# One cast and one subtraction per weight chunk, and GpSimd's elementwise work moved to VectorE and ScalarE, in a hybrid transformer block

## The chip, the core and the metric

The kernel runs on one core of a Trainium2 chip. The time is device microseconds of one execution. Its engines work in parallel, each through its own queue in order: TensorE (matmuls, and the loads of their stationary operand), VectorE, ScalarE, GpSimd, and SyncE, which here only issues transfers. In the profile they are PE and PEld, DVE, ACT, POOL and SP.

## What is computed

One layer on 256 tokens of width 2048, all in float32: a norm, one wide projection, four mixers (RWKV-7, RG-LRU, sparse attention "NSA", gated linear attention "GLA"), a gated sum of their outputs, an output projection with a residual, a second norm, and a feed-forward part with a causal convolution of three taps. In outline:

```
h = rms_norm(x);  p = h @ w_in
y_n = mixer_n(its columns of p)                      n = 0..3, each 256 x 512
m   = sum_n sigmoid(gate_n) * (y_n @ w_branch_n)     gate_n: 2048 columns of p
x2  = x + m @ w_out
u   = conv3(rms_norm(x2) @ w_up);  out = x2 + (silu(u1) * u2) @ w_down
```

The RWKV mixer needs, in each chunk of 64 tokens and each head, the inverse of a unit triangular matrix. It is solved by rows in two 32 x 32 blocks on each diagonal, and the corners are filled in by matmuls.

## The kernel before, in words

**The stream.** All activations are kept with channels on the 128 partitions and the 256 tokens along the free dimension. The weights (some 290 MB) are read once, in chunks of 128 x 1024 float32, each one transfer of 512 KB on SyncE's queue into a ring of five tiles `raw` (`stream`, line 300). A float32 product is made from rounded pieces: each weight is split into a high part `wh` and a low part `wl`. For each half chunk of 512 columns ScalarE casts `raw` to `wh` (line 327) and VectorE subtracts, `wl = raw - wh` (line 328). `wh` and `wl` are rings of six half chunks each (`BUFS`, line 1524). `stream` is a generator: it hands out blocks of 256 columns (512 in the three wide groups). The kernel does 1,096 such half chunks, in 548 chunks.

**The matmuls.** `group_A` takes 16 blocks or so (the contraction) and accumulates two tiles of 128 output channels in PSUM: for each block and tile one matmul of 512 columns with `wh` (both pieces of the activation) and one of 256 columns with `wl`. So a chunk of four blocks is 16 matmuls of 384 columns on average. Two accumulators of this kind alternate. Each group is then evacuated by ScalarE and VectorE (`fold`, `scaled`).

**The order.** The program order is: the projections of RWKV, its decay and solve (`rwkv_lora`, `rwkv_head`), the projections of RG-LRU and its recurrence (`lru`), the gates and branch products of RG-LRU (`merge(1, ...)`), with `rwkv_corners` called in the middle of them, after the third group of gates; then RWKV's chain of four chunks, GLA with its eight levels, its merge, NSA, the last two merges, the output projection, and the feed-forward part in three sections of 8, 7 and 7 units (`glu`), each followed by its part of `w_down`. A planner (the framework's, on modelled times) fixes the order of each engine's queue ahead of the run. It takes what is ready by priority: `load`, then `split`, then `evac`, then `mix` (all mixers' arithmetic), then `big` (the stream's matmuls); within a band in program order. `rwkv_corners` keeps its transpose of Z in program order on VectorE.

**GpSimd's share.** Helpers `tt` and `ts` run on VectorE unless given an engine. GpSimd gets:
- `rwkv_kk` (line 656): four scalings `kk` of 256 columns and the two products `k2` and `rk` of 1024 columns;
- `rwkv_blocks` (line 717): the solve, 31 steps of a product `ztmp` and a sum into `Z`, each of r x w columns with r = 31 - k, w = min(k + 1, 16) for k = 0..30, every one needing the one before. It begins with transfers of N (out to DRAM and back, on SyncE's queue) and ends with the store of `Z`, eight loads of `Zb` on the same queue and the transpose in `rwkv_corners`;
- `rwkv_chain` (line 820): the scaled state `sd`, in two of the four chunks;
- `gla` (line 1037): in each of eight levels one of the two products `qe` of 512 columns;
- `nsa` (line 1277): sixteen scalings of softmax rows `pt` of 128 or 256 columns;
- `branch` (line 1348): 24 additions of 512 columns into `merged`;
- and, not touched by the change, the sums of squares of the two norms (`norm_sum`), memsets, one-element copies ahead of loads, and some DMA issues.

Of the kernel before, what the change touches and what calls it, by code (L numbers as in the profile page):

```python
# [11 lines left out]
F32 = mybir.dt.float32  # L12
F32R = mybir.dt.float32r
U8 = mybir.dt.uint8
AF = mybir.ActivationFunctionType
ALU = mybir.AluOpType
MULT, ADD, SUB = ALU.mult, ALU.add, ALU.subtract
# [3 lines left out]
P = 128  # L21
# [204 lines left out]
class Kern:  # L226
# [73 lines left out]
    def stream(self, arr, c0, width, nblk):  # L300

        nc = self.nc
        nb, ns = 1024 // width, 512 // width
        for d in range(0, nblk, nb):
            if self.extras and not self.first and d % (self.every * nb) == 0:
                self.extras.pop(0)()
            self.nt += 1
            raw = self.pools["w"].tile([P, 1024], F32, tag="raw", bufs=BUFS["raw"], name=f"raw_{self.nt}")
            src = arr[c0 + d // nb]
            if self.first:  # L310
                with self.at("load"):
                    nc.sync.dma_start(raw[:, 0:512], src[:, 0:512])
                    nc.sync.dma_start(self.prm, self.A["prm"])
                self.extras.pop(0)()
                with self.at("load"):
                    nc.sync.dma_start(raw[:, 512:1024], src[:, 512:1024])
                self.first = False
            else:
                with self.at("load"):
                    nc.sync.dma_start(raw, src)  # L320
            for b in range(2):
                with self.at("split"):
                    self.nt += 1
                    wh = self.pools["w"].tile([P, 512], F32R, tag="wh", bufs=BUFS["wh"], name=f"wh_{self.nt}")
                    wl = self.pools["w"].tile([P, 512], F32R, tag="wl", bufs=BUFS["wl"], name=f"wl_{self.nt}")
                    rb = raw[:, b * 512:(b + 1) * 512]
                    nc.scalar.copy(wh, rb)  # L327
                    nc.vector.tensor_tensor(wl, rb, wh.bitcast(F32), op=SUB)  # L328
                for o in range(0, 512, width):
                    yield wh[:, o:o + width], wl[:, o:o + width]  # L330

    def acc(self):
        self.nt += 1
# [323 lines left out]
    def rwkv_kk(self):  # L657
        nc = self.nc
        hs = self.cst("hs")
        self.hs = hs  # L660
        kk = self.m4("kk")
        for j in range(4):
            nc.gpsimd.tensor_scalar(kk[:, j, :], self.rw_k[:, j, :], self.col("k_k", j), None, op0=MULT)
        sq = self.m4("kksq")
        self.act(sq, kk, AF.Square)

        def pre(out, ps):
            self.ts(out, ps, 1e-24, None, ALU.max)
            self.act(out, out, AF.Sqrt)

        def post(jp, pb):
            self.tt(kk[:, 2 * jp:2 * jp + 2, :], kk[:, 2 * jp:2 * jp + 2, :], pb, MULT)

        self.head_norm(sq, hs, pre, post)
        self.rw_kk = kk

        hka = self.sm([P, 4], "hka")
        self.ts(hka, self.col("k_a", 0, 4), 0.5, None, MULT)
        oka = self.sm([P, 4], "oka")
        self.ts(oka, hka, -1.0, 1.0, MULT, ADD)  # L680
        k2 = self.m4("k2")
        for j in range(4):
            self.act(k2[:, j, :], self.rw_tha[:, j, :], AF.Identity, scale=hka[:, j:j + 1], bias=oka[:, j:j + 1])
        self.tt(k2, k2, self.rw_k, MULT, nc.gpsimd)
        self.rw_k2 = k2
        bb = self.m4("bb")
        self.ts(bb, self.rw_tha, 0.5, 0.5, MULT, ADD)
        self.tt(bb, bb, kk, MULT)
        self.rw_b = bb
        rk = self.m4("rk")  # L690
        self.tt(rk, self.rw_r, k2, MULT, nc.gpsimd)
        self.rw_rk = rk

    def rwkv_ops(self, c):
# [19 lines left out]
    def rwkv_blocks(self, Ts):  # L714


        nc = self.nc
# [13 lines left out]
        nb = self.sb("mg", [P, 32, 32], F32, "N32")  # L731
        zb = self.m2("Z32", 32)
        tmp = self.m1("ztmp", 1)[:, 0, :]
        nc.sync.dma_start(self.flat(zb), self.A["z0"])
        for hf in range(2):
            for q in range(2):
                o = 64 * hf + 32 * q
                nc.sync.dma_start(nb[o:o + 32], nd.rearrange("u (a t) s -> (u a) t s", a=2)[:, 32 * q:32 * q + 32, 32 * q:32 * q + 32])
        for k in range(31):
            r, w = 31 - k, min(k + 1, 16)  # L740
            t = tmp[:, 0:r * w].rearrange("p (r w) -> p r w", r=r)
            self.tt(t, nb[:, k + 1:, k:k + 1].broadcast_to([P, r, w]), zb[:, k:k + 1, 0:w].broadcast_to([P, r, w]), MULT, nc.gpsimd)
            self.tt(zb[:, k + 1:, 0:w], zb[:, k + 1:, 0:w], t, ADD, nc.gpsimd)
        y = self.m4("Zb", 16)
        nc.gpsimd.memset(y, 0.0)
        nc.sync.dma_start(zd.rearrange("f q u a t s -> (f q u a) t s"), zb)
        for a in range(2):
            for q in range(2):
                for hf in range(2):
                    o, c0 = 64 * a + 32 * q, 32 * q + 16 * hf  # L750
# [67 lines left out]
    def rwkv_chain(self, c, T, st):  # L818
        nc = self.nc
# [19 lines left out]
        if c < 3:  # L839
            tk = T["tk"]  # L840
            ps = g4("S")
            for j in range(4):
                for par in range(2):
                    self.mm(ps[H[par], j, :], tk[:, par, j, :], uv[:, j, par, :])
            new = self.sb("st", [P, 4, 64], F32, "st")
            if st is None:
                nc.vector.tensor_copy(new, ps)
            else:
                sd = self.m1("sd")
                ec = self.rw_ec[:, :, c:c + 1]  # L850
                self.tt(sd, st, ec.broadcast_to([P, 4, 64]), MULT, nc.gpsimd)
                self.tt(new, sd, ps, ADD)
        ps = g4("Yo")
        for j in range(4):
# [182 lines left out]
    def gla(self):  # L1037
# [28 lines left out]
        for lv in range(8):  # L1066
# [6 lines left out]
            self.act(e, e, AF.Exp, scale=-1.0 / 16)  # L1073
            qe = self.m4("qe")
            self.tt(qe[:, 0:2, :], qk[:, 0:2, :], e, MULT)
            self.tt(qe[:, 2:4, :], qk[:, 2:4, :], e, MULT, nc.gpsimd)
            if lv == 6:
                for par in range(2):
                    h = H[par]
# [196 lines left out]
    def nsa(self):  # L1276
# [24 lines left out]
        for tt in range(2):  # L1301
# [19 lines left out]
            self.tt(lt, lt, ws[:, :, 0:1].broadcast_to([P, 4, 15]), MULT)  # L1321
            for h in range(4):
                for a in range(2):
                    nc.gpsimd.tensor_scalar(pts[h][:, a, :], pts[h][:, a, :], ws[:, h, 1 + a:2 + a], None, op0=MULT)
            srcs = [(None, 0)] + [(a, s) for a in range(2) for s in range(tt + 1)]
            po = self.ps("no")
            for n, (a, st) in enumerate(srcs):
# [24 lines left out]
    def branch(self, n, cg, h, yk, th, first):  # L1352
        ps = self.group_A(self.stream(self.A["w_branch"], (4 * n + cg) * 2 + h, 256, 4), 4, yk)
        with self.at("evac"):
            if first and h == 0:
                self.merged[cg] = self.sb("mg", [P, 4, 256], F32, f"merged{cg}")
            t, m = (v[:, 2 * h:2 * h + 2, :] for v in (th, self.merged[cg]))
            if first:
                self.fold(m, ps)
                self.stt(m, t, 1.0, m, ADD, MULT)  # L1360
            else:
                b = self.sb("fd", [P, 2, 256], F32, "b")
                self.fold(b, ps)
                self.stt(t, t, 1.0, b, ADD, MULT)
                self.tt(m, m, t, ADD, self.nc.gpsimd)

    def tick(self, most=0):

# [129 lines left out]
    def glu(self, g, up, h2):  # L1498
# [23 lines left out]


BAND = {"load": 0, "split": 1_000_000, "evac": 2_000_000, "mix": 3_000_000, "big": 4_000_000}
BUFS = {"raw": 5, "wh": 6, "wl": 6, "hh": 8, "m4": 8, "fd": 1, "ft": 3, "mg": 4, "yh": 2, "ops": 4, "m2": 4, "m1": 4, "st": 2, "bdr": 3,
        "pk": 1, "xa": 1, "xg": 1, "th": 2}


# [25 lines left out]
```

## Time and profile before

| what | value |
|---|---|
| three runs | 1599.86, 1607.89, 1608.23 us (median 1607.89) |
| the profiled execution | 1600.85 us, of which the profile's span is 1599.1 us |
| instructions | 27,514 |
| HBM read | 300.32 MB, 190 GB/s over the span |

The profile is of one execution. A busy share is the time in which an engine had at least one instruction running; matmuls overlap, and so do the ends and starts of neighbouring instructions on VectorE and ScalarE, so that an instruction's own duration is longer than the distance to the next start. "Idle before" is the time in which the engine stood still just ahead of an instruction, with what ended it. The granted clock is TensorE's, as a share of 2.4 GHz; 0.50 is its lower level of 1.2 GHz.

### The profile page before, as it was taken

The page shows a single profiled execution, that of the slowest core. Times are in us where ns is not written, and L with a number is a line of the kernel's source. Part 1 is how long each engine was busy: PE and PEld are TensorE (multiplying, and loading weights), DVE is VectorE, ACT ScalarE, POOL GpSimd, SP SyncE. Part 2 cuts the span into 40 slices and gives each one's busy share as a digit, 9 for nine tenths or more (in the row PEclk, how much of TensorE's full clock was granted, in tenths as well). Part 3 has the DMA queues.
Part 4 walks back from the last instruction along what each step waited for, and adds up shares of the span by engine and source line. Part 5 has one row for each costly group of instructions (what it writes and reads, how often), then busy time and mean ns, then how long its engine had stood idle before and what let it go on. Part 6 is the DMA issues. An engine that isn't in the chain of part 4 may idle for free.

```text
span 1599.1 us, 27514 instructions
## 1 busy us (share of the span) xinstructions
PE 1566.2 (98%) x10062; PEld 1414.7 (88%) x10062; DVE 1248.2 (78%) x2034; ACT 955.8 (60%) x1685; POOL 168.5 (11%) x178
## 2 busy tenths in 40 slices
PE   8999889999899999999999999999999999999998
PEld 7998778888789889899999999999999999999998
DVE  8798965485887768777797888886678886688875
ACT  6777543365665566656566666664466664566653
POOL 3113900000211201311121100000000000000000
PEclk9999988999999999999999999999999999999999
DMA  7656353256356766456676666666666666666663
GB/s 270 233 160 210 121 168 97 96 173 205 124 166 204 239 220 201 156 180 202 202 251 201 194 209 199 201 200 206 198 200 202 201 201 200 202 204 198 200 224 131
DMA packets 95801, 305.80 MB, mean 191 GB/s; under 512 B 20021, under 2 KB 20789, under 8 KB 95664
## 3 DMA queue, kind: packets, MB, share of 16 engines
q1 hardware_dynamic: 94448, 299.60, 58.3%
q0 software_dynamic: 1216, 4.43, 0.8%
q8 instruction: 79, 1.29, 0.3%
q14 instruction: 58, 0.48, 0.1%
HBM read 300.32 MB, written 3.67 MB: 190 GB/s over the span
## 4 chain that ended last, share of the span: by engine, by line
PE 89%; DVE 3%; POOL 3%; issue 2%; DMA 1%; ACT 1%; SPq 1%; DVEq 0%; POOLq 0%; ACTq 0%
PE acc L297 83%; POOL Z L289 2%; POOL ztmp L289 1%; DVE wl L328 1%; PE G L297 1%; PE Yo L297 1%; PE M L297 1%; DMA raw<-in_cmp 0%; PE no L297 0%; DMA raw<-in_wf_r 0%; ACT wh L327 0%; DVE qe L289 0%; PE r L297 0%; PE c L297 0%; PE sc L297 0%
## 5 line engine op out<-in xcount | busy, mean ns | idle before, releaser
L328 DVE TENSOR_TENSOR wl<-raw,wh 128x512 fp32r<-128x512 f32 x1096 | 788.1, 728 | 281.6 <-ACT wh L327 275.8
L297 PE MATMUL acc<-h,wh 128*128 128x512 f32 x3008 | 1000.3, 385 | 1.3 <-DVE th L289 0.9
L327 ACT CAST wh<-raw 128x512 fp32r<-128x512 f32 x1096 | 671.6, 619 | 507.3 <-PE acc L297 474.8
L297 PE MATMUL acc<-h,wl 128*128 128x256 f32 x3008 | 826.9, 275 | 6.1 <-DVE wl L328 6.1
L297 PEld LDWEIGHTS acc<-h,wh 128*128 128x128 f32 x3008 | 571.1, 190 | 83.5 <-issue 1.7
L297 PEld LDWEIGHTS acc<-h,wl 128*128 128x128 f32 x3008 | 579.9, 193 | 10.6 <-DVE wl L328 7.0
L297 PE MATMUL acc<-f,wh 128*128 128x512 f32 x704 | 230.7, 382 | 0.0
L297 PE MATMUL acc<-f,wl 128*128 128x256 f32 x704 | 191.9, 273 | 0.0
L297 PEld LDWEIGHTS acc<-f,wh 128*128 128x128 f32 x704 | 133.1, 189 | 18.5
L297 PEld LDWEIGHTS acc<-f,wl 128*128 128x128 f32 x704 | 135.2, 192 | 0.0
L297 PE MATMUL acc<-mg,wh 128*128 128x512 f32 x256 | 83.9, 382 | 0.3 <-DVE b L289 0.3
L286 DVE SCALAR_TENSOR_TENSOR u<-u,prm,u 128x254 f32<-128x254 f32 (+1 forms) x176 | 80.8, 480 | 0.5
L297 PE MATMUL acc<-mg,wl 128*128 128x256 f32 x256 | 69.6, 273 | 0.0
L289 POOL TENSOR_TENSOR merged<-merged,th 128x512 f32<-128x512 f32 x24 | 41.7, 1736 | 243.7 <-DVE th L286 243.7
L297 PEld LDWEIGHTS acc<-mg,wh 128*128 128x128 f32 x256 | 48.3, 189 | 7.3 <-DVE b L289 0.6
L289 DVE TENSOR_TENSOR xres<-xres,acc 128x512 f32<-128x512 f32 (+1 forms) x66 | 44.0, 668 | 9.9 <-PE acc L297 7.8
L283 ACT ACTIVATE u<-u,prm 128x256 f32<-128x256 f32 x88 | 48.1, 594 | 2.6 <-DVE u L289 0.8
L297 PEld LDWEIGHTS acc<-mg,wl 128*128 128x128 f32 x256 | 49.1, 192 | 0.1
L297 PE MATMUL acc<-wh,h 128*128 128x512 f32 (+1 forms) x128 | 30.2, 328 | 0.0
L289 DVE TENSOR_TENSOR u<-u,rs 128x512 f32<-128x512 f32 x44 | 30.1, 684 | 0.0
L289 DVE TENSOR_TENSOR u<-u,acc 128x512 f32<-128x512 f32 x44 | 30.0, 681 | 0.0
L283 ACT ACTIVATE th<-th 128x512 f32<-128x512 f32 (+1 forms) x33 | 21.3, 645 | 13.5 <-DVE th L289 12.4
(400 smaller groups left out, 1329.3 us busy)
## 6 DMA issues: line engine op xcount, KB each, us to landing
raw<-in_w_up SPq DMA_DIRECT2D x176, 512.0 KB, 4.3
raw<-in_w_gate SPq DMA_DIRECT2D x128, 512.0 KB, 3.6
raw<-in_w_down SPq DMA_DIRECT2D x88, 512.0 KB, 4.2
raw<-in_w_branch SPq DMA_DIRECT2D x32, 512.0 KB, 3.9
raw<-in_w_out SPq DMA_DIRECT2D x32, 512.0 KB, 4.2
raw<-in_wf_k SPq DMA_DIRECT2D x8, 512.0 KB, 4.4
raw<-in_wf_misc SPq DMA_DIRECT2D x8, 512.0 KB, 4.4
raw<-in_wf_lx SPq DMA_DIRECT2D x8, 512.0 KB, 4.3
```

The costliest lines, as they stand in the source:

```text
L283: return self.nc.scalar.activation(out, in_, func, bias=bias, scale=scale, **kw)
L286: return self.nc.vector.scalar_tensor_tensor(out, in0, scalar, in1, op0=op0, op1=op1)
L289: return (eng or self.nc.vector).tensor_tensor(out, a, b, op=op)
L297: return self.nc.tensor.matmul(out, lhsT, rhs, start=start, stop=stop, **kw)
L327: nc.scalar.copy(wh, rb)
L328: nc.vector.tensor_tensor(wl, rb, wh.bitcast(F32), op=SUB)
```

## The change

- `stream`: one cast and one subtraction of 1024 columns for each chunk (the very first chunk, which comes in two transfers, still in two halves). `wh` and `wl` become rings of three whole chunks: the same memory.
- `rwkv_kk`: `kk` on ScalarE, `k2` and `rk` on VectorE. `rwkv_blocks`, `rwkv_chain`, `gla`, `branch`: the same instructions on VectorE. `nsa`: the scalings on ScalarE.

```diff
--- before.py
+++ after.py
@@ -300,13 +300,14 @@
     def stream(self, arr, c0, width, nblk):
 
         nc = self.nc
-        nb, ns = 1024 // width, 512 // width
+        nb = 1024 // width
         for d in range(0, nblk, nb):
             if self.extras and not self.first and d % (self.every * nb) == 0:
                 self.extras.pop(0)()
             self.nt += 1
             raw = self.pools["w"].tile([P, 1024], F32, tag="raw", bufs=BUFS["raw"], name=f"raw_{self.nt}")
             src = arr[c0 + d // nb]
+            narrow = self.first
             if self.first:
                 with self.at("load"):
                     nc.sync.dma_start(raw[:, 0:512], src[:, 0:512])
@@ -318,16 +319,15 @@
             else:
                 with self.at("load"):
                     nc.sync.dma_start(raw, src)
-            for b in range(2):
-                with self.at("split"):
-                    self.nt += 1
-                    wh = self.pools["w"].tile([P, 512], F32R, tag="wh", bufs=BUFS["wh"], name=f"wh_{self.nt}")
-                    wl = self.pools["w"].tile([P, 512], F32R, tag="wl", bufs=BUFS["wl"], name=f"wl_{self.nt}")
-                    rb = raw[:, b * 512:(b + 1) * 512]
-                    nc.scalar.copy(wh, rb)
-                    nc.vector.tensor_tensor(wl, rb, wh.bitcast(F32), op=SUB)
-                for o in range(0, 512, width):
-                    yield wh[:, o:o + width], wl[:, o:o + width]
+            with self.at("split"):
+                self.nt += 1
+                wh = self.pools["w"].tile([P, 1024], F32R, tag="wh", bufs=BUFS["wh"], name=f"wh_{self.nt}")
+                wl = self.pools["w"].tile([P, 1024], F32R, tag="wl", bufs=BUFS["wl"], name=f"wl_{self.nt}")
+                for r in (slice(0, 512), slice(512, 1024)) if narrow else (slice(0, 1024),):
+                    nc.scalar.copy(wh[:, r], raw[:, r])
+                    nc.vector.tensor_tensor(wl[:, r], raw[:, r], wh[:, r].bitcast(F32), op=SUB)
+            for o in range(0, 1024, width):
+                yield wh[:, o:o + width], wl[:, o:o + width]
 
     def acc(self):
         self.nt += 1
@@ -660,7 +660,7 @@
         self.hs = hs
         kk = self.m4("kk")
         for j in range(4):
-            nc.gpsimd.tensor_scalar(kk[:, j, :], self.rw_k[:, j, :], self.col("k_k", j), None, op0=MULT)
+            self.act(kk[:, j, :], self.rw_k[:, j, :], AF.Copy, scale=self.col("k_k", j))
         sq = self.m4("kksq")
         self.act(sq, kk, AF.Square)
 
@@ -681,14 +681,14 @@
         k2 = self.m4("k2")
         for j in range(4):
             self.act(k2[:, j, :], self.rw_tha[:, j, :], AF.Identity, scale=hka[:, j:j + 1], bias=oka[:, j:j + 1])
-        self.tt(k2, k2, self.rw_k, MULT, nc.gpsimd)
+        self.tt(k2, k2, self.rw_k, MULT)
         self.rw_k2 = k2
         bb = self.m4("bb")
         self.ts(bb, self.rw_tha, 0.5, 0.5, MULT, ADD)
         self.tt(bb, bb, kk, MULT)
         self.rw_b = bb
         rk = self.m4("rk")
-        self.tt(rk, self.rw_r, k2, MULT, nc.gpsimd)
+        self.tt(rk, self.rw_r, k2, MULT)
         self.rw_rk = rk
 
     def rwkv_ops(self, c):
@@ -739,8 +739,8 @@
         for k in range(31):
             r, w = 31 - k, min(k + 1, 16)
             t = tmp[:, 0:r * w].rearrange("p (r w) -> p r w", r=r)
-            self.tt(t, nb[:, k + 1:, k:k + 1].broadcast_to([P, r, w]), zb[:, k:k + 1, 0:w].broadcast_to([P, r, w]), MULT, nc.gpsimd)
-            self.tt(zb[:, k + 1:, 0:w], zb[:, k + 1:, 0:w], t, ADD, nc.gpsimd)
+            self.tt(t, nb[:, k + 1:, k:k + 1].broadcast_to([P, r, w]), zb[:, k:k + 1, 0:w].broadcast_to([P, r, w]), MULT)
+            self.tt(zb[:, k + 1:, 0:w], zb[:, k + 1:, 0:w], t, ADD)
         y = self.m4("Zb", 16)
         nc.gpsimd.memset(y, 0.0)
         nc.sync.dma_start(zd.rearrange("f q u a t s -> (f q u a) t s"), zb)
@@ -848,7 +848,7 @@
             else:
                 sd = self.m1("sd")
                 ec = self.rw_ec[:, :, c:c + 1]
-                self.tt(sd, st, ec.broadcast_to([P, 4, 64]), MULT, nc.gpsimd)
+                self.tt(sd, st, ec.broadcast_to([P, 4, 64]), MULT)
                 self.tt(new, sd, ps, ADD)
         ps = g4("Yo")
         for j in range(4):
@@ -1073,7 +1073,7 @@
             self.act(e, e, AF.Exp, scale=-1.0 / 16)
             qe = self.m4("qe")
             self.tt(qe[:, 0:2, :], qk[:, 0:2, :], e, MULT)
-            self.tt(qe[:, 2:4, :], qk[:, 2:4, :], e, MULT, nc.gpsimd)
+            self.tt(qe[:, 2:4, :], qk[:, 2:4, :], e, MULT)
             if lv == 6:
                 for par in range(2):
                     h = H[par]
@@ -1321,7 +1321,7 @@
             self.tt(lt, lt, ws[:, :, 0:1].broadcast_to([P, 4, 15]), MULT)
             for h in range(4):
                 for a in range(2):
-                    nc.gpsimd.tensor_scalar(pts[h][:, a, :], pts[h][:, a, :], ws[:, h, 1 + a:2 + a], None, op0=MULT)
+                    self.act(pts[h][:, a, :], pts[h][:, a, :], AF.Copy, scale=ws[:, h, 1 + a:2 + a])
             srcs = [(None, 0)] + [(a, s) for a in range(2) for s in range(tt + 1)]
             po = self.ps("no")
             for n, (a, st) in enumerate(srcs):
@@ -1362,7 +1362,7 @@
                 b = self.sb("fd", [P, 2, 256], F32, "b")
                 self.fold(b, ps)
                 self.stt(t, t, 1.0, b, ADD, MULT)
-                self.tt(m, m, t, ADD, self.nc.gpsimd)
+                self.tt(m, m, t, ADD)
 
     def tick(self, most=0):
 
@@ -1522,7 +1522,7 @@
 
 
 BAND = {"load": 0, "split": 1_000_000, "evac": 2_000_000, "mix": 3_000_000, "big": 4_000_000}
-BUFS = {"raw": 5, "wh": 6, "wl": 6, "hh": 8, "m4": 8, "fd": 1, "ft": 3, "mg": 4, "yh": 2, "ops": 4, "m2": 4, "m1": 4, "st": 2, "bdr": 3,
+BUFS = {"raw": 5, "wh": 3, "wl": 3, "hh": 8, "m4": 8, "fd": 1, "ft": 3, "mg": 4, "yh": 2, "ops": 4, "m2": 4, "m1": 4, "st": 2, "bdr": 3,
         "pk": 1, "xa": 1, "xg": 1, "th": 2}
```

## Rows read from the trace of the kernel before

**Rows 1.** The page, busy us (share of the span) and instructions of each engine.

```profile
PE 1566.2 (98%) x10062; PEld 1414.7 (88%) x10062; DVE 1248.2 (78%) x2034; ACT 955.8 (60%) x1685; POOL 168.5 (11%) x178
```

**Rows 2.** Busy time of each engine by stretches.

```profile
core 0: us, PE busy (x) PEld busy (x) DVE busy (x) ACT busy (x) POOL busy (x), PEclk, DMA share, GB/s
...
150.00:200.00 50.00, 43.94 (x246) 39.38 (x245) 46.84 (x52) 30.99 (x56) 45.69 (x56) 0.93 0.41 131
200.00:215.00 15.00, 9.35 (x107) 8.41 (x106) 6.41 (x10) 4.68 (x9) 2.28 (x7) 0.79 0.75 215
240.00:320.00 80.00, 80.00 (x581) 66.29 (x580) 39.35 (x72) 28.77 (x54) 3.38 (x8) 0.89 0.30 96
400.00:450.00 50.00, 41.84 (x435) 36.43 (x427) 44.30 (x66) 32.95 (x60) 11.95 (x9) 1.00 0.36 119
690.00:920.00 230.00, 229.70 (x1403) 210.99 (x1402) 185.42 (x265) 140.99 (x242) 35.58 (x27) 1.00 0.64 208
920.00:1080.00 160.00, 160.00 (x979) 147.08 (x978) 138.99 (x239) 107.20 (x185) 0.00 (x0) 1.00 0.64 203
```

**Rows 3.** Timeline of GpSimd: start us, us, line, operation, tiles, shapes, count.

```profile
105.74 2.69 POOL L289 TENSOR_TENSOR rk<-rw_r,k 128x1024 f32<-128x1024 f32 x1
...
148.00 0.45 POOL L289 TENSOR_TENSOR ztmp<-N,Z 128x31 f32<-128x31 f32 x1 [16.09 <-DMA N<-n_rows]
...
200.73 0.55 POOL L289 TENSOR_TENSOR Z<-Z,ztmp 128x16 f32<-128x16 f32 x1
```

**Rows 4.** The chain that ended last, in order of time: start us, us, what.

```profile
201.30 2.09 DMA z_rows<-Z
207.44 3.25 DMA Zb<-z_rows
```

**Rows 5.** Waits of SyncE's queue: total us, times, longest.

```profile
SPq L746 <- POOL uv L792: 10.3, 1, 10.3
```

**Rows 6.** Timeline of VectorE: start us, us, line, operation, tiles, shapes, count [idle before].

```profile
8.75 0.55 DVE L286 SCALAR_TENSOR_TENSOR sm<-sm,sm 128x4 f32<-128x4 f32 x3
...
85.33 1.84 DVE L616 TENSOR_TENSOR_SCAN bcum<-cstt,lw 128x256 f32<-128x256 f32 x3
...
103.73 5.85 DVE L328 TENSOR_TENSOR wl<-raw,wh 128x512 fp32r<-128x512 f32 x3 [2.14 <-ACT wh L327]
...
122.89 1.21 DVE L289 TENSOR_TENSOR bb<-bb,kk 128x1024 f32<-128x1024 f32 x1
124.03 0.41 DVE L286 SCALAR_TENSOR_TENSOR ops<-kk,ein 128x252 f32<-128x252 f32 x1
...
127.84 0.41 DVE L289 TENSOR_TENSOR ops<-bb,eneg 128x256 f32<-128x256 f32 x1
128.18 0.41 DVE L289 TENSOR_TENSOR ops<-k,eneg 128x256 f32<-128x256 f32 x1
...
137.26 1.28 DVE L328 TENSOR_TENSOR wl<-raw,wh 128x512 fp32r<-128x512 f32 x2
...
211.08 1.25 DVE L758 STREAM_TRANSPOSE Z<-Zb 128x1024 f32<-128x1024 f32 x1 [8.56 <-DMA Zb<-z_rows]
```

**Rows 7.** Timeline of TensorE, columns as in rows 6.

```profile
175.57 0.58 PE L297 MATMUL acc<-h,wl 128*128 128x256 f32 x1 [4.86 <-DVE wl L328]
...
212.38 0.85 PE L297 MATMUL P<-Z,N 32*32 32x32 f32 x24 [5.65 <-DVE Z L758]
```

**Rows 8.** Subtractions wl in 150 to 200 us: duration ns least/median/most, starts.

```profile
L328 DVE TENSOR_TENSOR wl<-raw,wh x31: 677/955/1206, 150.7 to 199.2; 128x512 fp32r<-128x512 f32 x31
```

**Rows 9.** Products qe of the attention levels, columns as in rows 8.

```profile
L289 DVE TENSOR_TENSOR qe<-gqk,ge x8: 678/1236/1793, 411.5 to 447.1; 128x512 f32<-128x512 f32 x8
L289 POOL TENSOR_TENSOR qe<-gqk,ge x8: 1264/1279/1777, 411.6 to 447.1; 128x512 f32<-128x512 f32 x8
```

**Rows 10.** ScalarE: the casts by form (busy us, mean ns, idle before), then its timeline.

```profile
L327 ACT CAST wh<-raw 128x512 fp32r<-128x512 f32 x1096 | 671.6, 619 | 507.3 <-PE acc L297 474.8 <-DMA raw<-in_w_gate 6.0 <-ACT u L380 4.5
...
156.03 1.08 ACT L283 ACTIVATE a<-la 128x1024 f32<-128x1024 f32 x1
```

## The prediction

> **What bounds the kernel now.** I read the page's busy shares first. TensorE is busy 98% of the span, VectorE 78%, ScalarE 60%, GpSimd 11% [rows 1]. The span stands for an execution of 1600.85 us; the median of the three runs, 1607.89 us, is 7.0 us above it. My sum is made against 1600.85.
>
> Then the stretches, because an average hides where TensorE waits [rows 2]. From 690 us on there is nothing to win: in 920 to 1080 us TensorE is busy 160.00 of 160.00 us with 979 matmuls at a granted clock of 1.00, or 163.4 ns each, against 160 ns for the mean of 384 columns (512 and 256 alternating) at 2.4 GHz. In 690 to 920 us it is 229.70 of 230 us. More than half of the kernel is TensorE at its pace, and a faster split there only makes VectorE idle more.
>
> The time that can be won is ahead of that. In 150 to 200 us TensorE is busy 43.94 of 50 us, in 200 to 215 us 9.35 of 15 us, in 400 to 450 us 41.84 of 50 us. In the first of these GpSimd is busy 45.69 us and VectorE 46.84 us, and the granted clock is 0.93, then 0.79 [rows 2]: part of each stretch ran at the 1.2 GHz level, behind TensorE's idle time. That is 50 x 0.07 + 15 x 0.21 = 6.6 us of clock.
>
> What ends these waits: the 62 GpSimd instructions of the triangular solve run from 148.00 to 201.28 us [rows 3]; their result goes out and back by DMA, which is on the chain that ended last [rows 4]; the store of it held SyncE's queue for 10.3 us [rows 5], with weight loads queued behind it; then VectorE stood idle 8.56 us for the transpose of Z [rows 6], and TensorE 5.65 us for that transpose [rows 7]. Before that TensorE had waited 4.86 us for one subtraction [rows 7]. The subtractions are slow here: median 955 ns in 150 to 200 us, least 677 [rows 8]. So GpSimd sets the end of this stage twice: by its own length, and by slowing VectorE.
>
> **The change part by part.**
>
> *The solve.* Removed: 53.3 us of GpSimd. Added: 62 VectorE instructions that each need the one before. From the code their columns sum to 2 x 4,776 = 9,552 per partition. Bounds: two VectorE instructions of 256 columns start 0.34 us apart, and one of 1024 columns ends its turn after 1.14 us [rows 6], so a column costs about 1.04 ns and an instruction 0.07 us more. That gives 62 x 0.07 + 9.9 = 14.2 us if other work fills the dependence. Three dependent ones of 4 columns took 0.55 us [rows 6], about 0.19 each, which gives 62 x 0.19 + 9.9 = 21.7 us if nothing does. I take 18, the middle, since the planner has subtractions to put between for about half of them.
>
> [...]
>
> VectorE's own work in 150 to 200 us without GpSimd beside it: the 31 subtractions [rows 8] at 0.60 (two take 1.28 us, so the second adds 0.60 [rows 6]) are 18.6 us; the other 21 are 4 of 1024 columns at 1.14, 11 at 0.60, 2 at 0.40 and 4 scans at 0.59 (three took 1.84 us where GpSimd was idle [rows 6]), 14.3 us. Together 32.9 of the 46.84 us measured: 13.9 us were waiting for GpSimd. With the solve it is 32.9 + 18 = 51 us, 47 to 55 by the bounds. So VectorE is as full as before, not emptier. The gain is elsewhere: before, VectorE was full to 202 us and then idle for 8.56 us. The solve comes ahead of the recurrence's arithmetic in the order of priorities, so it should be done some 10 us before VectorE's other work, and the DMA round trip (201.30 to 211.08 us) lies beside that work. It also starts earlier: at 103 to 109 us three subtractions took 5.85 us beside the GpSimd products k2 and rk [rows 3, 6], 4.0 over the 1.9 they need; the two products cost VectorE 2 x 1.14. Net 1.7 us. Sum 8.6 + 1.7, I take **10 us**. Bounds: nothing, if the solve is dear and ends last; 4.9 + 5.7 + 6.6 = 17 us, if every wait and all the clock come back. What is late next is VectorE itself, and TensorE will still wait for a subtraction or two.
>
> *Queues passed.* SyncE's queue keeps the store and the eight loads of Z; only the wait ahead of them shortens. GpSimd keeps memsets, small copies and its own DMA issues, with nothing long in front.
>
> *The gated linear attention, eight levels.* A product of 128x512 moves from GpSimd (1.28 us) to VectorE. In each level one VectorE instruction beside it took up to 1.79 us instead of 0.68 [rows 9]. Removed 8 x 1.1 = 8.8 us of waiting, added 8 x 0.60 = 4.8 us, net 4.0 us on VectorE, which is busy 44.30 of 50 us there while TensorE idles 8.2 [rows 2]. I take **4 us**; bounds 0 and 8.2.
>
> *The merge.* 24 additions, 14.4 us on VectorE, against as many waits of up to 1.1 us. They lie in 455 to 826 us, beside a TensorE that is full: nothing either way. If that cover were gone it would cost the 14.4 us. The same holds for the two state products.
>
> *On ScalarE.* Four scalings of kk (256 columns) and sixteen of the softmax rows, each under the 0.62 us of a 512-column cast [rows 10]: at most 12 us on an engine that is idle 40% of the time [rows 1]; nothing on the path, the 12 us if uncovered.
>
> *One cast and one subtraction per chunk.* 548 chunks, less one. A subtraction of 1024 columns takes 1.14 us of VectorE instead of 1.20, a cast 1.08 instead of at most 1.24 [rows 6, 10]: about 33 us of VectorE in all, of which 50 us of the dense stretch hold 19 x 0.06 = 1.1 us. The price: TensorE gets the first half of a chunk only after the whole of it, about 0.46 + 0.52 = 1 us later. In a full ring that is hidden. Where TensorE is already waiting (the start, the solve, the attention levels) I charge 1 us each, **3 us**; bounds 0 and 6.
>
> Sum: 1600.85 - 10 - 4 + 3 = 1589.9 us. A median of several runs may lie up to 7 us above its profiled execution, as it does here; I add half and say 1593 us.
>
> **The rivals.**
>
> *The solve still ends last.* If the planner puts the solve's instructions behind the recurrence's, or VectorE's 55 us apply, Z is ready at 148 - 1.7 + 55 and the round trip of 10 us follows with nothing beside it: 211.6 us, as before. For it: VectorE is the full engine of the stage. Against: the order of priorities. Then only 4 - 3 us are left: 1600 us, with the same half, 1603.
>
> *The coarse ring stalls the dense part; slower.* The casts wait for TensorE to release a ring slot (474.8 us in all [rows 10]). Now three slots hold a chunk each: from a release TensorE has two chunks left, 2 x 16 matmuls x 163.4 ns = 5.2 us. Cast 1.08, subtraction 1.21, and one other instruction ahead on each engine, 0.62 + 0.69: 3.6 us, so it holds. It decides once another 1.6 us is queued ahead, as it could be in the 22 gated units of the last half, where ScalarE and VectorE each have runs of evacuation work. At 1 us per unit: 1589.9 + 22 = 1612 us. For it: the slack was six halves with 1.3 us hand-offs. Against: priorities put splits ahead of evacuation.
>
> *That the change doesn't do what it says* is hardly open: the edits name the engines and sizes themselves.
>
> **How the numbers follow.** A measurement can tell 0.5%, about 8 us, from no change. The forecast has a chance of 0.60; within it a gain of 11 us with bounds of some 6 either side passes 8 us three times in four. The first rival has 0.22, no measurable change. The second 0.18, nearly all slower. Faster 0.45, same 0.38, slower 0.17. The range: low end 1600.85 - 17 - 8.2, about 1575; high end the second rival with the 3.5 us for the median, about 1615. The forecast's own range is 1582 to 1604.
>
> **What would show it.** Right: the subtractions of the dense stretch at 1.21 us with no GpSimd beside them; the solve on VectorE in 15 to 22 us of busy time, done by about 190 us; SyncE's wait of 10.3 us and VectorE's 8.56 us gone; TensorE's 920 to 1080 us stretch still full. Wrong: Z transposed at 211 us or later; TensorE idle for more than a few us after 690 us; another stretch of granted clock near 0.5, as 240 to 320 us has now (0.89 [rows 2]), growing with the longer hand-offs. A gain far above 17 us would mean that the waits of the first 100 us, which I leave as they are, depend on the split too.

## The result, and the profile after

The changed kernel takes 1588.99 us (median of four runs, 1585.32 to 1593.95) against 1608.06 for the kernel before in the same session (four runs, 1599.86 to 1610.69): ratio 0.9894, interval 0.9872 to 0.9915. The forecast was 1593. The profiled execution took 1589.25 us, 11.6 less than the 1600.85 of before; the sum had given 11. (The medians lie 19 us apart, since the profiled execution of before is 7 us below its median and that of after is not.) The granted clock moved as well: its mean is 0.988 in the profiled execution of before and 0.993 in that of after, and 0.012 x 1599.1 less 0.007 x 1587.5 is 8 us. By this estimate up to 8 of the 11.6 us are clock. The total was right; two of its parts were not, and their errors cancel.

The page's first part, beside [rows 1]: GpSimd is nearly empty, and VectorE is busy for less time, not more.

```profile
PE 1563.9 (99%) x10062; PEld 1408.5 (89%) x10062; DVE 1178.8 (74%) x1585; ACT 876.3 (55%) x1158; POOL 44.3 (3%) x60
```

The same kernel by stretches, beside [rows 2] (columns: stretch and its length, busy time of each engine with instructions, granted clock, DMA share, GB/s):

```profile
core 0: us, PE busy (x) PEld busy (x) DVE busy (x) ACT busy (x) POOL busy (x), PEclk, DMA share, GB/s
150.00:200.00 50.00, 49.00 (x298) 44.63 (x297) 49.15 (x85) 30.96 (x37) 0.00 (x0) 1.00 0.61 196
200.00:215.00 15.00, 14.62 (x90) 13.21 (x89) 9.22 (x15) 7.76 (x10) 0.61 (x2) 1.00 0.74 208
240.00:320.00 80.00, 80.00 (x608) 65.70 (x607) 37.32 (x57) 25.85 (x42) 2.08 (x6) 0.91 0.33 108
385.00:435.00 50.00, 46.98 (x485) 40.53 (x482) 45.43 (x69) 37.48 (x53) 1.38 (x3) 1.00 0.48 152
690.00:920.00 230.00, 227.26 (x1373) 206.52 (x1373) 167.62 (x192) 125.83 (x155) 18.59 (x15) 1.00 0.64 206
920.00:1080.00 160.00, 160.00 (x978) 147.22 (x977) 129.89 (x171) 94.89 (x119) 0.00 (x0) 1.00 0.63 198
```

In 150 to 200 us TensorE is busy 49.00 of 50 us instead of 43.94, at clock 1.00 instead of 0.93, and makes 298 matmuls instead of 246. VectorE is as full as the prediction said, 49.15 us. The attention levels now lie some 15 us earlier, so 385 to 435 stands against 400 to 450 of before: idle time 3.0 us instead of 8.2. The dense part in 920 to 1080 is as full as it was. But 690 to 920, full before, has lost 2.4 us and 30 matmuls. That is new.

The slow subtractions and the held queue of [rows 8] and [rows 5] are gone. The subtraction's tile in 150 to 200 us of after (count: least, median and greatest ns, first and last start):

```profile
L328 DVE TENSOR_TENSOR wl<-raw,wh x19: 1193/1216/1226, 150.5 to 198.0; 128x1024 fp32r<-128x1024 f32 x19
```

Two of SyncE's waits in 140 to 225 us of after, the first those of the weight loads, the second that of the solve's store (engine and line, released by: us, times, longest):

```profile
SPq L321 <- DVE wl L328: 20.2, 9, 5.5
...
SPq L746 <- DVE merged L286: 1.1, 1, 1.1
```

A whole chunk of 1024 columns now takes 1216 ns, where half of it, 512 columns, took 955 before. The store of the solve holds SyncE 1.1 us, not 10.3. But the solve itself is not early. VectorE's timeline of after around its end (start, us, instruction; idle time before it and what ended it):

```profile
204.36 0.17 DVE L289 TENSOR_TENSOR Z<-Z,ztmp 128x16 f32<-128x16 f32 x1
...
216.99 1.25 DVE L758 STREAM_TRANSPOSE Z<-Zb 128x1024 f32<-128x1024 f32 x1 [4.06 <-DMA Zb<-z_rows]
```

TensorE's timeline of after where it takes Z up:

```profile
215.65 0.27 PE L297 MATMUL acc<-yb,wl 128*128 128x256 f32 x1
218.29 0.38 PE L297 MATMUL P<-Z,N 32*32 32x32 f32 x12 [2.37 <-DVE Z L758]
```

The solve ends at 204.5 us, 3.3 us later than on GpSimd [rows 3], though it began 5.6 us sooner (142.4 against 148.0 us): it takes 62 us instead of 53. Z is transposed 5.9 us later than before [rows 6]. Yet TensorE waits for it only 2.37 us instead of 5.65. The windows from the first product of RG-LRU's branch (yb) to the corners (P) show why. In the kernel before:

```profile
196.77:212.38 15.61, 9.96 (x62) 8.82 (x60) 7.01 (x11) 5.74 (x10) 5.13 (x11) 0.88 0.58 150
```

The same stretch in the kernel after:

```profile
185.03:218.29 33.26, 29.51 (x178) 26.39 (x177) 24.77 (x48) 16.66 (x20) 0.61 (x2) 1.00 0.66 200
```

The planner has put the corners later in TensorE's queue: 178 instructions stand between these two points instead of 62. At 163.4 ns a matmul, the 116 more are 19 us of dense work, done in the time in which Z is on its way.

Where the time came from, by the start of the same matmul in each trace (us; `gz` is the first of the attention levels, `yd` the branch product of GLA's merge, `mg` the output projection, `f` the feed-forward part). The labels are those of the experiments below. Each row is one execution. In e2 again and e8 every one of TensorE's, VectorE's and ScalarE's instructions stands in the same order as in e2, and in e5 as in after, so these rows show how far two executions of one order lie apart: up to 4 us.

| kernel | first yb | P | gz | last yd | first mg | first f |
|---|---|---|---|---|---|---|
| before | 196.8 | 212.4 | 398.4 | 551.6 | 818.5 | 1070.5 |
| after | 185.0 | 218.3 | 383.8 | 533.9 | 806.9 | 1058.9 |
| e5, as after | 183.0 | 216.3 | 381.7 | 531.9 | 806.0 | 1058.1 |
| e2, engines alone | 184.3 | 224.9 | 378.2 | 530.4 | 798.2 | 1050.2 |
| e2 again | 187.0 | 228.6 | 381.3 | 533.4 | 800.1 | 1052.2 |
| e8, as e2 | 184.0 | 224.5 | 377.9 | 530.1 | 796.6 | 1048.6 |
| e6, halves in merges | 184.7 | 221.5 | 379.8 | 531.1 | 800.6 | 1052.7 |
| e3, solve alone | 189.4 | 228.0 | 392.0 | 546.5 | 813.7 | 1065.8 |
| e4, all but the solve | 194.6 | 211.2 | 404.8 | 555.8 | 822.6 | 1074.6 |
| e9, idle solve | 201.9 | 245.0 | 397.2 | 549.4 | 817.1 | 1069.1 |

After leads before by 14.6 us when attention starts and by 17.7 at the end of GLA's merge. It loses 6.1 of that by the output projection, and nothing changes from there to the end.

### The profile page after: what moved, and what is told of

Read it like the earlier page. It is cut to its first block, busy times and chain, and to the rows that moved or that the text cites. A ratio compares the mean times of both kernels' runs of the same rounds, so it can differ in the third digit from the quotient of the medians.

```text
span 1587.5 us, 25427 instructions
## 1 busy us (share of the span) xinstructions
PE 1563.9 (99%) x10062; PEld 1408.5 (89%) x10062; DVE 1178.8 (74%) x1585; ACT 876.3 (55%) x1158; POOL 44.3 (3%) x60
## 3 DMA queue, kind: packets, MB, share of 16 engines
q0 software_dynamic: 1216, 4.43, 0.7%
## 4 chain that ended last, share of the span: by engine, by line
PE 88%; DVE 6%; ACT 3%; issue 2%; DMA 1%; SPq 0%; DVEq 0%; ACTq 0%
PE acc L297 82%; DVE wl L328 3%; ACT wh L327 2%; PE G L297 1%; DVE th L289 1%; PE Yo L297 1%; PE M L297 0%; PE no L297 0%; DMA raw<-in_wf_r 0%; DMA raw<-in_cmp 0%; PE c L297 0%; DVE Z L289 0%; DMA Zb<-z_rows 0%; DMA z_rows<-Z 0%; PE ptp L1332 0%
## 5 line engine op out<-in xcount | busy, mean ns | idle before, releaser
L328 DVE TENSOR_TENSOR wl<-raw,wh 128x1024 fp32r<-128x1024 f32 (+1 forms) x549 | 673.3, 1228 | 327.6 <-ACT wh L327 316.6
L327 ACT CAST wh<-raw 128x1024 fp32r<-128x1024 f32 (+1 forms) x549 | 574.3, 1048 | 595.6 <-PE acc L297 498.4
L286 DVE SCALAR_TENSOR_TENSOR u<-u,prm,u 128x254 f32<-128x254 f32 (+1 forms) x176 | 73.0, 477 | 0.0
L380 ACT COPY u<-acc 128x512 f32<-128x512 f32 x44 | 25.4, 577 | 0.0
```

The lines of the kernel that those rows point to most:

```text
L286: return self.nc.vector.scalar_tensor_tensor(out, in0, scalar, in1, op0=op0, op1=op1)
L327: nc.scalar.copy(wh[:, r], raw[:, r])
L328: nc.vector.tensor_tensor(wl[:, r], raw[:, r], wh[:, r].bitcast(F32), op=SUB)
L380: self.nc.scalar.copy(dst, ps[0:rows, :, 0])
```

## The experiments

Each run stands as a ratio against the kernel before on the same chip.

### The two halves of the change

e1 has only the new `stream` (as in the change above) and its rings, e2 only the moved operations with the half chunks of before. The rings in e1:

```diff
-BUFS = {"raw": 5, "wh": 6, "wl": 6, ...
+BUFS = {"raw": 5, "wh": 3, "wl": 3, ...
```

> Only the split by whole chunks, GpSimd's work as before. Theory (the coarse subtraction delays the release of an accumulator in the merges, some 0.45 us in each of about 20 pairs of gates and branch product, and GpSimd's work is the gain): slower than before by 6 to 12 us, so 1.004 to 1.008 of it, with TensorE idle ahead of the next gates in each pair. Rival (the coarse split is harmless or a small gain): 0.998 to 1.001.

> Only GpSimd's elementwise work moved, casts and subtractions by half chunks as before. Theory: faster than the full change by the 8 to 10 us that the coarse split gives back, so 0.982 to 0.985 of before. Rival (the two parts help each other): 0.989 to 0.993.

e1: 1.0016 (0.9995 to 1.0037), 1608.88 us: between the two theories, and not decided by its median. e2: 0.9834 (0.9807 to 0.9861), 1580.38 us; run again in another session, 0.9845 (0.9821 to 0.9870), 1582.27 us. So the moved operations gain 1.6%, 25 to 26 us, and the coarse split takes back some 8 us of it where the sum charged 3. The runs differ in the granted clock too. Over the 43 runs of before beside the experiments the time falls by about 1.3 us for each 0.001 of mean granted clock (from 1613.21 us at 0.982 to 1596.81 at 0.993). An estimate from that rate, for a clock of 0.990: before 1601.7 us, after 1593.1, e1 1610.1, e2 1582.6 and 1583.4. Then e1 is 8 us slower than before, as its theory said, e2 is 18 to 19 faster and after 9. How much of a kernel's clock is its own doing was not separated.

In e2 the stretch that went soft is full (windows of e2):

```profile
690.00:920.00 230.00, 230.00 (x1405) 211.39 (x1404) 184.75 (x287) 144.12 (x246) 14.67 (x15) 1.00 0.67 209
```

### The moved operations, taken apart

e3 moves the solve alone, e4 all but the solve.

```diff
 # e3
-            self.tt(t, nb[:, k + 1:, k:k + 1].broadcast_to([P, r, w]), zb[:, k:k + 1, 0:w].broadcast_to([P, r, w]), MULT, nc.gpsimd)
-            self.tt(zb[:, k + 1:, 0:w], zb[:, k + 1:, 0:w], t, ADD, nc.gpsimd)
+            self.tt(t, nb[:, k + 1:, k:k + 1].broadcast_to([P, r, w]), zb[:, k:k + 1, 0:w].broadcast_to([P, r, w]), MULT)
+            self.tt(zb[:, k + 1:, 0:w], zb[:, k + 1:, 0:w], t, ADD)
```

> Before, with only the 62 instructions of the solve on VectorE. Theory (nearly all of the gain is the solve's): faster by 12 to 16 us, 0.990 to 0.9925 of before, with the 4.86 us wait for a subtraction gone. Rival (the other moved work carries a part as large): 0.994 to 0.998.

> All moved work except the solve, which stays on GpSimd; half chunks. Theory: 2 to 5 us faster than before (the attention levels), 0.997 to 0.999. Rival: 0.988 to 0.993 if the many small moves carry the gain.

e3: 0.9920 (0.9886 to 0.9955). e4: 0.9976 (0.9949 to 1.0002), which can't be told from no change. Both lie in the range of their theory. In e4 the solve's stage is as it was before: its subtractions, by tile in 150 to 200 us, are as slow as those of [rows 8].

```profile
L328 DVE TENSOR_TENSOR wl<-raw,wh x30: 680/992/1126, 150.5 to 198.9; 128x512 fp32r<-128x512 f32 x30
```

So the solve is the larger part. The two make 17 us together, e2 makes 26. The missing 9 us lie in the granted clock, by the same estimate: at 0.990 e3 takes 1590.7 us and e4 1594.2, gains of 11.0 and 7.5, which together are the 18 to 19 of e2. Their median clocks are 0.987 (e3) and 0.982 (e4), against 0.986 for before and 0.992 for e2. In 240 to 320 us it is 0.80 in e3 and 0.79 in e4 against 0.89 in e2, and 0.09 of 80 us is 7 us. Why it differs there, where small matmuls of the RWKV chain and dense ones alternate, was not tried; e2 again, the same program, has 0.94.

### Is it the company of GpSimd, or the end of the solve?

e8 is e2 with the solve in a band of priority of its own ahead of the splits. e9 is e2 with a copy of the solve on GpSimd besides, into scratch that nobody reads: the solve's real end no longer depends on GpSimd, only its company is back.

```diff
 # e8, around the two lines of the solve, and in the bands
+            with self.at("free"):
...
-BAND = {"load": 0, "split": 1_000_000, "evac": 2_000_000, "mix": 3_000_000, "big": 4_000_000}
+BAND = {"load": 0, "free": 500_000, "split": 1_000_000, "evac": 2_000_000, "mix": 3_000_000, "big": 4_000_000}
 # e9
+        tmp2, z2 = self.sm([P, 256], "tmp2"), self.sm([P, 32, 16], "z2")
+        nc.gpsimd.memset(z2, 0.0)
...
+            t2 = tmp2[:, 0:r * w].rearrange("p (r w) -> p r w", r=r)
+            self.tt(t2, nb[:, k + 1:, k:k + 1].broadcast_to([P, r, w]), z2[:, k:k + 1, 0:w].broadcast_to([P, r, w]), MULT, nc.gpsimd)
+            self.tt(z2[:, k + 1:, 0:w], z2[:, k + 1:, 0:w], t2, ADD, nc.gpsimd)
```

> GpSimd's work moved with half chunks, and the solve given a priority ahead of the split, so that it ends some 30 us earlier. Theory (the end of the solve is not what bounds; the gain was VectorE's slowed subtractions and SyncE's held queue): within 0.4% of the version with the same engines, 0.980 to 0.988 of before. Rival (the end of the solve and its DMA round trip still bound the stage): 8 to 12 us less than that version, 0.975 to 0.978.

> GpSimd's work moved with half chunks, and beside the real solve a copy of it on GpSimd on scratch data, whose result nothing reads. Theory (GpSimd slows the VectorE instructions that run beside it): the subtractions in 150 to 200 us back near 0.95 us, TensorE waiting for them again, 6 to 14 us more than without, 0.987 to 0.992 of before. Rival (GpSimd's end was the limit, not its company): no more than 2 us, 0.981 to 0.985.

e8: 0.9852 (0.9806 to 0.9898), as e2. The last instruction of its solve starts at 210.8 us against 211.2, and its queues are those of e2, instruction for instruction: the edit moved nothing and says nothing on what an earlier end is worth. e9: 0.9946 (0.9922 to 0.9971), 1598.31 us, 17 us above e8 in the same session and 18 above e2 (14 to 15 at a clock of 0.990, by the estimate above). All queues but GpSimd's hold the same instructions in the same order as in e2, so it is not a new order that costs the time. Company alone takes back two thirds of e2's gain, more than was expected of it. The subtraction's tile in 150 to 200 us, in e2:

```profile
L328 DVE TENSOR_TENSOR wl<-raw,wh x38: 664/682/691, 149.4 to 198.8; 128x512 fp32r<-128x512 f32 x38
```

The same in e9:

```profile
L328 DVE TENSOR_TENSOR wl<-raw,wh x25: 676/943/1191, 150.7 to 199.9; 128x512 fp32r<-128x512 f32 x25
```

The window of that stretch in e9:

```profile
150.00:200.00 50.00, 37.88 (x207) 32.23 (x206) 49.79 (x65) 25.18 (x44) 44.84 (x61) 0.97 0.38 117
```

VectorE is busy 49.79 us, as in e2 (49.64), but gets through 25 subtractions there instead of 38, and TensorE makes 207 matmuls instead of 294.

So a subtraction of a half chunk, which reads two tiles, takes 682 ns (median) in e2, where GpSimd does nothing in this stretch, and 943 in e9, where it is busy 44.84 of the 50 us. What in the two engines makes it so is not shown by these runs.

e11 asks whether the same holds for the last of GpSimd's elementwise work too, the norm's sums, which the change leaves there. It is e2 with one more line changed.

```diff
-        g = nc.gpsimd
+        g = nc.vector
```

> GpSimd's work moved with half chunks, and the additions of the norms' sums of squares on VectorE as well (they run on GpSimd beside the first 35 us). Theory (GpSimd slows VectorE's two-input instructions there as well, and VectorE is full in 10 to 35 us): 1 to 4 us less than without, 0.980 to 0.983 of before. Rival (VectorE is full, so 11 more instructions cost what the company did): 0.983 to 0.986.

e11: 0.9812 (0.9787 to 0.9838), 1577.18 us against 1582.27 for e2 on the same chip: the fastest version of all. VectorE's timeline at the start of e2:

```profile
26.10 5.70 DVE L328 TENSOR_TENSOR wl<-raw,wh 128x512 fp32r<-128x512 f32 x3
```

The same point in VectorE's timeline of e11:

```profile
24.35 2.50 DVE L328 TENSOR_TENSOR wl<-raw,wh 128x512 fp32r<-128x512 f32 x4
```

Three subtractions took 5.70 us beside GpSimd's sums, four take 2.50 without. In the first 40 us VectorE is busy 31.42 us in e11 against 34.20 in e2, though it was given the sums. The sums themselves are shorter on VectorE too (0.69 to 0.70 us for 512 columns and 0.42 to 0.43 for 256 in e11, against 1.27 to 1.57 and 0.71 to 1.06 on GpSimd in e2, 23.5 to 31.3 us), and e11's queues stand in another order; what part of the 5 us is company was not separated.

### What the coarse split costs, and where

The waits view of after, 440 to 830 us, has a group that e2 does not have:

```profile
PEld acc L297 <- DVE th L289: 8.6, 15, 0.7
...
PE acc L297 <- DVE th L289: 4.2, 15, 0.4
```

One such place, on TensorE's timeline of after:

```profile
757.02 0.27 PE L297 MATMUL acc<-h,wl 128*128 128x256 f32 x1
757.13 0.38 PE L297 MATMUL acc<-yc,wh 128*128 128x512 f32 x1
...
759.64 0.27 PE L297 MATMUL acc<-yc,wl 128*128 128x256 f32 x1
760.17 0.48 PE L297 MATMUL acc<-h,wh 128*128 128x512 f32 x1 [0.27 <-DVE th L289]
```

On VectorE's timeline of after:

```profile
758.30 1.22 DVE L328 TENSOR_TENSOR wl<-raw,wh 128x1024 fp32r<-128x1024 f32 x1 [1.40 <-ACT wh L327]
759.44 0.68 DVE L289 TENSOR_TENSOR th<-th,acc 128x512 f32<-128x512 f32 x1
```

On ScalarE's timeline of after:

```profile
757.22 1.05 ACT L327 CAST wh<-raw 128x1024 fp32r<-128x1024 f32 x1 [1.57 <-PE acc L297]
758.17 0.58 ACT L380 COPY th<-acc 128x512 f32<-128x512 f32 x1
```

A group of gates ends its matmuls as the branch product begins (757.13). That product is one chunk, 16 matmuls or 2.6 us, and after it TensorE wants the gates' accumulator back. The accumulator comes free when VectorE has added its second half to `th`. But the cast starts only when TensorE has given back a ring slot (the 1.57 us of ScalarE's idle time), VectorE idles until the whole cast is done, then does the whole subtraction, then the addition: 757.13 to 760.12 us, 3.0 us. TensorE starts 0.42 us later than it could: 0.53 us after the last matmul of 256 columns, where 0.11 is usual (757.02 to 757.13). TensorE's timeline has 17 such places between 461 and 807 us, 0.42 to 0.58 us each, 7.5 us in all. (The waits view of TensorE counts less, 4.2 us, since it starts from the end of the last matmul.)

Four edits of after: e5 puts the gates' evacuation ahead of the splits in priority; e6 returns to halves in the merges' weights alone, in the ring of whole chunks; e7 does so everywhere; e12 keeps the whole cast and halves only the subtraction.

```diff
 # e5
-            self.scaled(t, ps)
+            with self.at("free"):
+                self.fold(t, ps)
+            self.tt(t, t, self.rs4[:, 0:2, :], MULT)
 # e6
-            narrow = self.first
+            narrow = self.first or arr.tensor.name in ("in_w_gate", "in_w_branch")
 # e7
+            narrow = True
 # e12
+                    for q in (r,) if narrow else (slice(0, 512), slice(512, 1024)):
+                        nc.vector.tensor_tensor(wl[:, q], raw[:, q], wh[:, q].bitcast(F32), op=SUB)
```

> The full change, but the evacuation that frees a gates accumulator (copy and addition) is given a priority ahead of casts and subtractions. Theory (in the merges the accumulator waits behind one whole cast and one whole subtraction): the 0.45 us waits ahead of the gates vanish, some 8 us less than the full change, 0.982 to 0.986 of before. Rival (the loss is in the ring of three slots): within 0.2% of the full change, 0.988 to 0.991.

> The full change, but with two casts and two subtractions of 512 columns in the streams of the gates and the branch products alone; tiles and rings stay whole chunks. Theory (the length of one instruction is what delays the accumulator): 0.982 to 0.986 of before, and the dense part as full as before. Rival (the ring of three slots is the cause): as the full change, 0.988 to 0.991.

> The full change, with two casts and two subtractions of 512 columns in every chunk, in tiles and rings of whole chunks. Theory (the length of one instruction is the whole price of the coarse split; the ring of three slots costs nothing): within 0.2% of the version with rings of half chunks, 0.982 to 0.985 of before, no waits ahead of the gates. Rival (releasing a slot only by whole chunks costs too): 0.986 to 0.990.

> The full change, with one cast of 1024 columns but two subtractions of 512. It tells the cast's part of the wait from the subtraction's. Theory (the copy waits behind the cast on ScalarE, the addition behind the subtraction on VectorE, each by about 0.5 us, and the whole cast also delays the first half's subtraction): about half of the waits of 0.45 us stay, 0.985 to 0.988 of before. Rival (one of the two is all of it): 0.982 to 0.985 if the subtraction, 0.988 to 0.991 if the cast.

> GpSimd's work moved with half chunks, a second time and on the same chip as its neighbours here: 0.981 to 0.986 of before.

e2 again: 0.9845, as given above, inside its range.

e5: 0.9887 (0.9843 to 0.9931), and the same two lines of waits, 8.6 and 4.2 us. The priority did not change the order: the queues are those of after, instruction for instruction. So e5 says nothing on the cause, for or against. That the planner found cast and subtraction ready first is a guess.

e6: 0.9863 (0.9819 to 0.9906), 1583.40 us, just above its theory's range. The waits view of e6 in 440 to 830 us shrinks:

```profile
PEld acc L297 <- DVE th L289: 4.4, 15, 0.8
...
PE acc L297 <- DVE th L289: 1.1, 3, 0.5
```

And the window of e6 fills:

```profile
690.00:920.00 230.00, 229.60 (x1392) 209.37 (x1391) 172.06 (x235) 131.88 (x195) 18.60 (x15) 1.00 0.66 207
```

By the table e6 reaches the output projection 6.3 us ahead of after, of the 8.7 us that e2 is ahead. Where it gains them is less sure, since e5, with after's order, lies 2 us from after at the start of attention. Steadier is the stretch from the last `yd` to the first `mg`, in which the two last merges lie: 273.0 and 274.1 us in after and e5, 266.5 to 267.8 in e2, e2 again and e8, 269.5 in e6. There e6 recovers some 4 of 6.5 us; five of the 17 places are left, 2.5 us. Its interval overlaps that of after; the profiles, not the medians, carry this. At a clock of 0.990 it takes 1586.3 us by the estimate above, 7 less than after.

e7: 0.9898 (0.9848 to 0.9947). That is in its rival's range (the release of a slot by whole chunks costs too), with an interval that reaches the theory's. From the last `yd` to the first `mg` it takes 269.5 us, as e6 does, and TensorE's waits for `th` are down to 0.9 us. But at a clock of 0.990 it takes 1592.5 us, as after does: by that estimate it loses elsewhere what it gains in the merges. Some 400 matmuls in, it is 4 us behind e2 (80.3 against 76.3 us), but e2 again is 2 us behind as well (78.6). What the ring of three whole chunks costs outside the merges is open.

e12: 0.9888 (0.9868 to 0.9908), 1590.35 us, no better than after: the range named for the cast. TensorE's waits for `th` grow from 4.2 to 7.1 us. VectorE's timeline of e12 at one of the merges shows why:

```profile
755.64 1.29 DVE L329 TENSOR_TENSOR wl<-raw,wh 128x512 fp32r<-128x512 f32 x2 [1.32 <-ACT wh L327]
756.85 0.68 DVE L289 TENSOR_TENSOR th<-th,acc 128x512 f32<-128x512 f32 x1
```

ScalarE's timeline of e12 at that place:

```profile
754.56 1.05 ACT L327 CAST wh<-raw 128x1024 fp32r<-128x1024 f32 x1 [1.57 <-PE acc L297]
```

Both halves of the subtraction wait for the whole cast, and the addition waits for both. What half chunks buy is that VectorE can subtract the first half while ScalarE casts the second. With the cast whole, shorter subtractions gain nothing; shorter casts with a whole subtraction were not run.

## Why the prediction was right, and where it was not

*What bounds the kernel.* Right. All that was won lies ahead of 690 us, and 920 to 1080 us did not move.

*The solve, 10 us.* The sign was right and the mechanism half right. That GpSimd's company slows VectorE is shown (e9: 943 ns for a subtraction of a half chunk against 682 in e2), the 4.86 us wait and SyncE's 10.3 us are gone, and VectorE is as full as forecast. The 6.6 us of clock, which only the upper bound held and not the 10, came back as well: in before the granted clock was 0.50 in 175 to 181 and in 209 to 218 us, in after it was 1.00 throughout 150 to 215 us. The solve's 62 instructions (window of after for the tile `ztmp`, which each of them reads or writes):

```profile
140.00:206.00 66.00, 19.51 (x62) 1.00 0.60 194
```

That is 19.5 us, between the two bounds and above the 18 taken. The step that failed is "The solve comes ahead of the recurrence's arithmetic" and "done by about 190 us": VectorE works at both together and ends the solve at 204.5 us. This is the first rival's place, and "Z transposed at 211 us or later" was named as a sign of being wrong. Its price did not follow, because the corners moved back in TensorE's order by 19 us of dense work. The stage gave 14.6 us by the start of attention, after the coarse split's own loss there; e2, without that loss, gave 20.2, and 17.1 and 20.5 in the two other executions of its order. Both took in the earlier work of `k2` and `rk`. So the bound of 17 us was reached without the split, and twice passed.

*The attention levels, 4 us.* TensorE's idle time there fell by 5.1 us, and from `gz` to the last `yd` the lead grew by 3.1 us: about the size. In e2 it grew by 1.0 us only, at a granted clock of 0.98 in that stretch, where before and after have 1.00.

*The merge's additions, nothing.* From the last `yd` to the output projection e2 takes 267.8 us against 266.9 before: nothing, as said.

*The coarse split, 3 us.* Mis-sized and put in the wrong place. The sum charged 1 us each at the start, the solve and the attention levels; the cost is 8.7 us by the table (after against e2 at `mg`), and the part of it that is located, some 6.5 us from the last `yd` to `mg`, lies in the merges, where e6 recovers 4. They were taken as covered: "In a full ring that is hidden" looks only at the matmul that waits for the weights. The one that waits for its accumulator, behind the same cast, was not looked for: 7.5 us in 17 places. The second rival (a coarse ring that stalls the dense part) was right that dense work stalls. It put the loss in the 22 gated units, and there nothing is lost: from the first `f` to the end of the span it is 1587.5 less 1058.9 us in after and 1599.1 less 1070.5 before, 528.6 both. It is the merges, whose branch product lasts one chunk, that have too little between two uses of an accumulator.

By the profiled executions the moves gave 20.3 us (1600.85 less 1580.53 in e2) where the sum had 14, and the split took 8.7 where it had 3: six too little on either side, and so a total that was right partly by luck. At a clock of 0.990, by the estimate above, the moves give 18 to 19 us, the split takes about 10, and 9 are left where the sum had 11. The sum without the split's 3 us gives 1586.9 for e2, which took 1580.53.

## What to carry to other kernels

Here an engine that is busy 11% cost a great deal by the company it kept (17 us for the idle copy of the solve in e9): look at what the full engine's instructions take beside it and without it, before counting what moving the work will add. When a split of work between two engines is made coarser, ask not only whether the consumer's ring holds, but what else stands behind the longer instruction in each queue, above all what frees an accumulator, and how much work lies between two uses of it. Compare runs with their granted clock beside them: here half of the difference in the medians can be clock. And where a planner orders the queues, a later result may cost nothing, because its consumer moves too (here Z came 5.9 us later, and TensorE waited 2.37 us for it instead of 5.65): compare how many instructions stand ahead of the consumer, not only when the result arrives.

## What the runs showed of the hardware beyond this

The company's price was larger than expected: e9 lost 17 to 18 us to instructions whose result nobody reads, with single subtractions of 512 columns at up to 1191 ns against 691 at most in e2.

Among the small matmuls of the RWKV chain the granted clock falls to 0.50 for a while in before and in after (mean 0.51 and 0.69 in 270 to 283 us). Its mean over 240 to 320 us is 0.79 to 0.91 in e1, e2, e3, e4, e6 and e11, and 0.97 to 0.99 in e7, e9 and e12. In TensorE's timeline of after a 512-column matmul takes 0.63 us there, where the granted clock is 0.50 (276 to 284 us), and 0.38 where it is 1.00:

```profile
276.52 0.63 PE L297 MATMUL acc<-h,wh 128*128 128x512 f32 x1
...
277.73 0.48 PE L297 MATMUL G<-uv,mt 128*64 128x64 f32 x2
278.13 0.47 PE L297 MATMUL G<-st,ops 64*64 64x64 f32 x2
```

In after, six dense matmuls in a row, 2304 columns together, take 1.92 us from the first start to the next one behind them at 0.50 (221.65 to 223.57 us), which is 1.2 columns in a nanosecond; at 1.00 the 163.4 ns for 384 columns on average are 2.35. So the 1.2 GHz ahead of the result is the rate measured at 0.50, one column taken as one cycle; 2.4 GHz and the 160 ns are an estimate, at twice that rate. What lowers the clock is not shown: TensorE is busy 80.00 of 80.00 us in 240 to 320 us.

The change neither caused nor cured the fall (0.91 in 240 to 320 us against 0.89), and one program varies as much between two executions (0.89 in e2, 0.94 in e2 again).
